# A two-layer hybrid decoder on one core: two of the four weight sums of a Strassen block by accumulating DMAs, ten such blocks, reordered projections, 512-column first up blocks

## The chip, the cores and the metric

One Trainium2 chip, of which the kernel uses one core. The metric is the device time of one execution in microseconds. The kernel before was timed in three runs: 949.24 us median, 949.19 to 950.22.

## The reference

Two decoder layers on a sequence of 256 tokens (T) with 1024 features (D), all in float32. Each layer ends with the MLP that most of the change touches:

```python
for l in range(DEPTH):                                 # DEPTH = 2
    u = rms_norm(h, norm_mix_pre[l])
    proj = u @ w_in[l]                                 # 1024 x 7680: q, k, v, xr, yr, pp, gates
    q, k, v, xr, yr, pp, gt = jnp.split(proj, SPLITS, axis=-1)
    ...                                                # attention, RG-LRU on xr and yr, pooling of pp, gates
    mix = merged @ w_out[l]
    h = h + rms_norm(mix, norm_mix_post[l])
    m = rms_norm(h, norm_mlp_pre[l])
    y = jnp.square(jax.nn.relu(m @ w_mlp_up[l])) @ w_mlp_down[l]     # 1024 -> 4096 -> 1024
    h = h + rms_norm(y, norm_mlp_post[l])
```

## The kernel before, in words

**Split products.** Every float32 product runs on TensorE as three products in a faster format (fp32r): high by high, high by low, low by high. `split` (L88 to L95) makes the two parts of a tile: ScalarE copies it rounded (L90, the high part), VectorE subtracts that from the source (L91, the low part). So each weight passes DMA, ScalarE and VectorE before TensorE reads it.

**Weights.** All large weights are laid out by the host as units of 128 x 1024 floats (512 KB) in the order of use, `wts`. `load_to` (L136) issues their loads on the SP queue (L140) into a ring of NRAW = 7 raw tiles; `split_to` splits them into rings of 8 high and 8 low tiles. The instructions are recorded in program order, with a few jobs put off by `later` and `tick` and some given a high priority; the tile scheduler then orders each engine's queue. An engine runs its queue in order.

**The projections.** pp, yr and xr take four units of work each per layer. `w_unit2` (L285 to L304) does one: two PSUM banks, each with eight matmuls of 512 columns (high weights against both parts of u, L299 and L302) and eight of 256 columns (low weights, L300). The 512 columns are two pieces of 256 in the tile `u2`.

**The MLP's up projection** is cut into 16 blocks of 256 hidden features. `up_first` (L733) does the first two with tokens as rows: per half of the tokens and per block `by_pass` (L330 to L339) runs 24 matmuls of 256 columns (L337), and the result is transposed into `zs`. Between its matmuls `mlp_in(1)` puts the transposes (L222) that bring the second half of the tokens into the feature layout. The other 14 blocks go through `up` (L764): `w_unit`, 48 matmuls of 256 columns (L98 to L100), relu and square.

**The MLP's down projection** has a block of 256 hidden features (two units of weights) for each up block. The first `nstr` = NBLK - PLAIN = 8 blocks use Strassen's form (Winograd's variant) for a 2 x 2 by 2 x 2 split: seven products of half size instead of eight. Seven PSUM banks collect the seven products over all blocks. For each block VectorE makes four sums of hidden pieces (`hidden_forms`, L777 to L780) and four sums of weight pieces (`weight_sums`): L794 adds the left half of the second unit to both halves of the first (1024 wide), L798 and L799 go on from there (512 wide each). Then `weight_forms` splits the four sums (`sh`, `sl`), and `down` runs 21 matmuls of 512 columns. UPS says how many up units stand ahead of each block's products: (2, 2, 2, 1, 2, 1, 2, 1). The other 8 blocks are plain: 24 matmuls of 512 columns each (`plain`); the last three of them (LAST) run together at the end. The weight sums lie in a tile of the `acts` pool under the tag "lo", which has two buffers.

Of the kernel before, what the change touches and what calls it, by code (L numbers as in the profile page):

```python
# [9 lines left out]
F32 = mybir.dt.float32  # L10
# [3 lines left out]
ALU = mybir.AluOpType  # L14
PSUM = bass.MemoryType.PSUM

L = 2
D = 1024
T = 256
P = 128  # L20
# [16 lines left out]
PLAIN = 8  # L37
LAST = 3

UPS = (2, 2, 2, 1, 2, 1, 2, 1)  # L40
NBLK = 16
# [17 lines left out]
def trunk(ctx, tc, x, wts, rgw, par, gpost, eye, ctab, out):  # L59
# [72 lines left out]

    per_layer = NHU // L
    fine = {i + l * per_layer for l in range(L) for i in [*range(FINE[0]), *range(per_layer - 64, per_layer - 64 + FINE[1])]}

    def load_to(n):  # L136
        while st["load"] < min(n, NHU):
            i = st["load"]
            r = raws.tile([P, HU_COLS], F32, tag="raw", name=f"raw{i}")
            nc.sync.dma_start(r[:], wts[i])  # L140
            raw_t[i] = r
            st["load"] += 1
# [144 lines left out]
    def w_unit2(hus, x2):  # L287


        banks = []  # L290
        for n in range(2):
            ps = bank([P, 2, T])
            for i, (wh, wl) in enumerate(hus):
                a = wh.rearrange("p (k n) -> p k n", k=4)
                b = wl.rearrange("p (k n) -> p k n", k=4)
                for k in range(4):
                    c = 4 * i + k
                    if c < 7:
                        PE.matmul(ps[:], a[:, k, n * P:(n + 1) * P], x2[:, :, c, :], start=c == 0, stop=False)  # L299
                    PE.matmul(ps[:, 0, :], b[:, k, n * P:(n + 1) * P], x2[:, 0, c, :], start=False, stop=False)  # L300
                    if c == 7:
                        PE.matmul(ps[:], a[:, k, n * P:(n + 1) * P], x2[:, :, c, :], start=False, stop=True)  # L302
            banks.append(ps)
        return banks  # L304
# [63 lines left out]
    for l in range(L):  # L368
# [361 lines left out]
        nstr = NBLK - PLAIN  # L730
        prods = {}
        zs, forms, wforms = {}, {}, {}

        def up_first():

            hus = take(4)
            toks = []
            for j in range(2):
                zs[j] = ttile([P, 2, T], nm="z")

            def hidden_T(tt):
                p2 = bank([P, 4, P])
                for j in range(4):
                    PE.transpose(p2[:, j, :], toks[tt][:, j * P:(j + 1) * P], ident)
                for j in range(2):
                    A.activation(zs[j][:, :, tt * P:(tt + 1) * P], p2[:, 2 * j:2 * j + 2, :], AF.Copy)

            for tt in range(2):
                ps = bank([P, 512])
                for u in range(2):  # L750
                    w = [[t_.rearrange("p (k n) -> p k n", k=4)[:, k, :] for hu in hus[2 * u:2 * u + 2]
                          for k in range(4) for t_ in hu[i:i + 1]] for i in range(2)]
                    by_pass(ps[:, u * 256:(u + 1) * 256], uh, ul, w[0], w[1], tt,
                            mid=(lambda: mlp_in(1)) if tt == 0 and u == 1 else None)
                z = ttile([P, 512], nm="zt")
                A.activation(z[:], ps[:], AF.Relu)
                V.tensor_tensor(out=z[:], in0=z[:], in1=z[:], op=ALU.mult)
                toks.append(z)
            later(1, lambda: hidden_T(0))
            later(1, lambda: hidden_T(1))  # L760
# [25 lines left out]

        def weight_sums(j):

            load_to(st["split"] + 2)
            r0, r1 = raw_t.pop(st["split"]), raw_t.pop(st["split"] + 1)  # L790
            st["split"] += 2
            st["use"] += 2
            t8 = acts.tile([P, 4, 512], F32, tag="lo", name="wsum")
            V.tensor_tensor(out=t8[:, 0:2, :], in0=r0.rearrange("p (b n) -> p b n", b=2),  # L794
                            in1=r1[:, 0:512].unsqueeze(1).to_broadcast([P, 2, 512]), op=ALU.add)
            w1 = (his.tile([P, HU_COLS], F32R, tag="wh", name="dh"), los.tile([P, HU_COLS], F32R, tag="wl", name="dl"))
            w4 = (ttile([P, 512], F32R, nm="bh"), ttile([P, 512], F32R, nm="bl"))
            V.tensor_tensor(out=t8[:, 2, :], in0=t8[:, 0, :], in1=r0[:, 512:1024], op=ALU.add)  # L798
            V.tensor_tensor(out=t8[:, 3, :], in0=t8[:, 2, :], in1=r1[:, 512:1024], op=ALU.add)  # L799
            split(w1[0][:], w1[1][:], r0[:])  # L800
            split(w4[0][:], w4[1][:], r1[:, 512:1024])
            wforms[j] = [w1, w4, t8]
            load_to(st["split"] + NRAW - 2)

        def weight_forms(j):
            t8 = wforms[j].pop()
            for i in range(2):
                w = (his.tile([P, HU_COLS], F32R, tag="wh", name="sh"), los.tile([P, HU_COLS], F32R, tag="wl", name="sl"))
                split(w[0][:], w[1][:], t8[:, 2 * i:2 * i + 2, :].rearrange("p b n -> p (b n)"))
                wforms[j].append(w)  # L810
# [12 lines left out]

        up_first()
        split_to(st["use"] + 2)
# [6 lines left out]
        for j in range(nstr):  # L832
            for i in range(UPS[j]):
# [110 lines left out]
def _layout(i):  # L944
    qc = np.concatenate([np.arange(hd * 64, hd * 64 + 64) for hd in _HEADS])
    units, rg, par, gp = [], [], [], []
    for l in range(L):
# [21 lines left out]
        units += [up[0], up[1], up[2], pairs[0], up[3]]  # L969
# [43 lines left out]
```

## Time and profile before

| | |
|---|---|
| median of three runs | 949.24 us |
| the profiled execution's own time | 949.69 us |
| its span | 947.9 us |
| TensorE (PE) busy | 936.9 us, 99% of the span |
| VectorE (DVE) busy | 751.6 us, 79% |
| ScalarE (ACT) busy | 624.9 us, 66% |
| GpSimd (POOL) busy | 2.0 us |
| weight loads on the SP queue | 316 of 512 KB, 4.4 us from issue to landing |

The profiled execution's time is 1.8 us more than its span, which begins with the first and ends with the last recorded work. A row of the profile names line, engine, operation and the tiles written and read. The durations of TensorE's rows overlap, since matmuls are pipelined: what one costs in a run is the distance between two starts.

### The profile page before, as it was taken

What the parts mean: (1) busy time and instruction counts of PE and PEld (TensorE: products, weight loads), DVE (VectorE), ACT (ScalarE), POOL (GpSimd) and SP (SyncE); (2) the same over time, 40 slices, a digit from 0 to 9 for tenths busy, and PEclk for the clock granted to TensorE, in tenths of its full rate; (3) what the DMA queues carried; (4) which work ended last, traced back from release to release, by engine and by line L of the source; (5) the groups of instructions that cost most, each with busy time, mean ns of one, the idle gap of its engine ahead of it and who ended that gap; (6) DMA issues with size and microseconds to landing.
All of it is one profiled execution on the core that took longest, in us unless ns stands there. A gap on an engine that the chain in (4) does not pass through costs nothing.

```text
span 947.9 us, 14352 instructions
## 1 busy us (share of the span) xinstructions
PE 936.9 (99%) x5284; PEld 805.1 (85%) x5284; DVE 751.6 (79%) x1321; ACT 624.9 (66%) x1079; POOL 2.0 (0%) x20
## 2 busy tenths in 40 slices
PE   8999999999999999999999999999999999999997
PEld 5888977888888999998878888888888899999985
DVE  6878886879868988886596788786897599889753
ACT  8655765679737777675375666656995478676731
POOL 0000000000000000000000000000000000000000
PEclk9999999999999999999999999999999999999998
DMA  8764454543754655566457545545438265656621
GB/s 321 275 213 160 134 182 163 194 159 125 268 176 154 215 178 189 200 201 221 134 182 259 165 144 181 184 140 192 155 125 287 100 221 184 230 171 200 214 72 44
DMA packets 48742, 173.24 MB, mean 183 GB/s; under 512 B 5408, under 2 KB 5792, under 8 KB 48672
## 3 DMA queue, kind: packets, MB, share of 16 engines
q1 hardware_dynamic: 48384, 172.16, 54.4%
q8 instruction: 41, 0.67, 0.3%
q14 instruction: 29, 0.24, 0.1%
q10 hardware_dynamic: 288, 0.17, 0.1%
HBM read 171.26 MB, written 1.05 MB: 182 GB/s over the span
## 4 chain that ended last, share of the span: by engine, by line
PE 98%; ACT 1%; DMA 1%; DVE 0%; issue 0%; SPq 0%; DVEq 0%
PE ps L98 17%; PE ps L100 17%; PE ps L99 17%; PE ps L337 9%; PE ps L299 8%; PE pr L98 6%; PE pr L99 6%; PE pr L100 6%; PE ps L300 5%; PE ps L425 1%; PE ps L473 1%; PE ps L302 1%; PE ps L462 1%; PE ps L222 1%; DMA raw<-wts 1%; PE ps L405 0%
## 5 line engine op out<-in xcount | busy, mean ns | idle before, releaser
L91 DVE TENSOR_TENSOR wl<-raw,wh 128x1024 fp32r<-128x1024 f32 (+1 forms) x312 | 344.8, 1124 | 78.1 <-ACT wh L90 69.7
L90 ACT ACTIVATE wh<-raw 128x1024 fp32r<-128x1024 f32 (+1 forms) x312 | 296.3, 987 | 145.6 <-PE ps L100 47.3
L98 PE MATMUL ps<-m,wh 128*128 128x256 f32 x448 | 126.8, 283 | 0.0
L100 PE MATMUL ps<-m,wl 128*128 128x256 f32 x448 | 126.8, 283 | 0.0
L99 PE MATMUL ps<-m,wh 128*128 128x256 f32 x448 | 126.7, 283 | 0.0
L299 PE MATMUL ps<-u,wh 128*128 128x512 f32 x336 | 121.1, 399 | 0.0
L300 PE MATMUL ps<-u,wl 128*128 128x256 f32 x384 | 99.9, 281 | 0.0
L98 PEld LDWEIGHTS ps<-m,wh 128*128 128x128 f32 x448 | 85.9, 192 | 1.0
L99 PEld LDWEIGHTS ps<-m,wh 128*128 128x128 f32 x448 | 85.9, 192 | 0.9
L100 PEld LDWEIGHTS ps<-m,wl 128*128 128x128 f32 x448 | 85.9, 192 | 0.0
L98 PE MATMUL ps<-wh,u 128*128 128x512 f32 x200 | 78.5, 393 | 0.5 <-ACT u L228 0.5
L100 PE MATMUL ps<-wh,u 128*128 128x512 f32 x200 | 78.0, 390 | 0.4 <-DVE u L230 0.4
L99 PE MATMUL ps<-wl,u 128*128 128x512 f32 x200 | 78.0, 390 | 0.0
L300 PEld LDWEIGHTS ps<-u,wl 128*128 128x128 f32 x384 | 72.5, 189 | 3.8
L299 PEld LDWEIGHTS ps<-u,wh 128*128 128x128 f32 x336 | 63.2, 188 | 14.2 <-issue 0.7
L98 PE MATMUL pr<-wh,hid 128*128 128x512 f32 x128 | 49.9, 390 | 0.0
L100 PE MATMUL pr<-wh,hid 128*128 128x512 f32 x128 | 49.8, 389 | 0.0
L99 PE MATMUL pr<-wl,hid 128*128 128x512 f32 x128 | 49.8, 389 | 0.0
L90 ACT ACTIVATE sh<-wsum 128x1024 fp32r<-128x1024 f32 x32 | 33.8, 1057 | 23.6 <-PE ps L99 20.5
L91 DVE TENSOR_TENSOR sl<-wsum,sh 128x1024 fp32r<-128x1024 f32 x32 | 38.9, 1222 | 11.7 <-ACT sh L90 11.3
L98 PEld LDWEIGHTS ps<-wh,u 128*128 128x128 f32 x200 | 37.5, 188 | 8.9 <-ACT u L228 0.7
L100 PEld LDWEIGHTS ps<-wh,u 128*128 128x128 f32 x200 | 37.5, 188 | 8.7 <-DVE u L230 0.9
(233 smaller groups left out, 1929.1 us busy)
## 6 DMA issues: line engine op xcount, KB each, us to landing
raw<-wts SPq DMA_DIRECT2D x316, 512.0 KB, 4.4
gB<-gpost SPq DMA_DIRECT2D x4, 512.0 KB, 5.5
rg<-rgw SPq DMA_DIRECT2D x8, 256.0 KB, 4.4
out<-h SPq DMA_DIRECT2D x4, 256.0 KB, 2.0
h<-x SPq DMA_DIRECT2D x2, 256.0 KB, 3.4
h<-x SPq DMA_DIRECT2D x1, 512.0 KB, 6.9
cst<-ctab SPq DMA_DIRECT2D x1, 168.0 KB, 7.0
prm<-par ACTq DMA_DIRECT2D x1, 104.0 KB, 3.8
```

The lines of the kernel that those rows point to most:

```text
L90: A.activation(hi, src, AF.Copy)
L91: V.tensor_tensor(out=lo, in0=src, in1=hi.bitcast(F32), op=ALU.subtract)
L98: PE.matmul(o, lh, rh, start=start, stop=False, **kw)
L99: PE.matmul(o, lh, rl, start=False, stop=False, **kw)
L100: PE.matmul(o, ll, rh, start=False, stop=stop, **kw)
L222: PE.transpose(banks[c // 4][:, c % 4, :], src[c // 4][:, (c % 4) * P:(c % 4 + 1) * P], ident)
L299: PE.matmul(ps[:], a[:, k, n * P:(n + 1) * P], x2[:, :, c, :], start=c == 0, stop=False)
L300: PE.matmul(ps[:, 0, :], b[:, k, n * P:(n + 1) * P], x2[:, 0, c, :], start=False, stop=False)
L302: PE.matmul(ps[:], a[:, k, n * P:(n + 1) * P], x2[:, :, c, :], start=False, stop=True)
L337: PE.matmul(o, xx[:, c, tsl], ww[c], start=(n == 0 and c == 0), stop=(n == 2 and c == 7))
L425: PE.matmul(sc[hd // hp][:, hd % hp, :], qT[a, j // 2][rows, j % 2, blk * P:(blk + 1) * P], kTs[0][rows, a, 0:w], start=True, stop=True)
L462: PE.transpose(ps[:, g, :], g8["p"](4 * b + g)[:, kt * P:(kt + 1) * P], ident)
```

## The change

- **Ten Strassen blocks** in a layer instead of eight (PLAIN 8 to 6); UPS becomes (2, 1, 1, 2, 1, 1, 2, 1, 1, 1), and the layout of the weights follows.
- **`dma_sums`**: for two blocks at a time, GpSimd's DMA queue loads the first unit of each into a tile `dsum` (L794) and then adds the left half of the second unit to both of its halves by a DMA with an add (L796). This takes the place of the 1024-wide add on VectorE. The tile is under the tag "lo", two buffers. It is called before and after `up_first` and at the start of every odd block for the pair three blocks on.
- The second unit's raw load brings its right half alone (256 KB); the two 512-wide sums (now L811, L812) go into a tile from the raw ring.
- **`w_unit2`** runs the eight matmuls of 512 columns of a bank first and the eight of 256 columns behind them.
- **`up_first`** runs one `by_pass` of 512 columns for each half of the tokens, with weights laid out for that; `mlp_in(1)` stays at the second matmul of the last pass of the first half.

```diff
@@ -34,10 +34,10 @@
-PLAIN = 8
+PLAIN = 6
 LAST = 3
 
-UPS = (2, 2, 2, 1, 2, 1, 2, 1)
+UPS = (2, 1, 1, 2, 1, 1, 2, 1, 1, 1)
@@ -130,6 +130,11 @@
+    nstr = NBLK - PLAIN
+    pair_at = [[(l + 1) * (NHU // L) - 64 + 6 + 2 * j + 2 * (sum(UPS[:j - 1]) + 1 if j else 0) for j in range(nstr)]
+               for l in range(L)]
+    half = {i + 1 for at in pair_at for i in at}
+
@@ -137,7 +142,10 @@
         while st["load"] < min(n, NHU):
             i = st["load"]
             r = raws.tile([P, HU_COLS], F32, tag="raw", name=f"raw{i}")
-            nc.sync.dma_start(r[:], wts[i])
+            if i in half:
+                nc.sync.dma_start(r[:, 512:1024], wts[i][:, 512:1024])
+            else:
+                nc.sync.dma_start(r[:], wts[i])
             raw_t[i] = r
             st["load"] += 1
 
@@ -290,16 +298,12 @@
         banks = []
         for n in range(2):
             ps = bank([P, 2, T])
-            for i, (wh, wl) in enumerate(hus):
-                a = wh.rearrange("p (k n) -> p k n", k=4)
-                b = wl.rearrange("p (k n) -> p k n", k=4)
-                for k in range(4):
-                    c = 4 * i + k
-                    if c < 7:
-                        PE.matmul(ps[:], a[:, k, n * P:(n + 1) * P], x2[:, :, c, :], start=c == 0, stop=False)
-                    PE.matmul(ps[:, 0, :], b[:, k, n * P:(n + 1) * P], x2[:, 0, c, :], start=False, stop=False)
-                    if c == 7:
-                        PE.matmul(ps[:], a[:, k, n * P:(n + 1) * P], x2[:, :, c, :], start=False, stop=True)
+            ws = [[hu[i].rearrange("p (k n) -> p k n", k=4)[:, k, n * P:(n + 1) * P] for hu in hus for k in range(4)]
+                  for i in range(2)]
+            for c in range(8):
+                PE.matmul(ps[:], ws[0][c], x2[:, :, c, :], start=c == 0, stop=False)
+            for c in range(8):
+                PE.matmul(ps[:, 0, :], ws[1][c], x2[:, 0, c, :], start=False, stop=c == 7)
             banks.append(ps)
         return banks
 
@@ -727,13 +731,14 @@
 
-        nstr = NBLK - PLAIN
-        prods = {}
+        prods, t8s = {}, {}
         zs, forms, wforms = {}, {}, {}
 
         def up_first():
 
             hus = take(4)
+            w = [[t_.rearrange("p (k n) -> p k n", k=2)[:, k, :] for hu in hus for k in range(2) for t_ in hu[i:i + 1]]
+                 for i in range(2)]
             toks = []
             for j in range(2):
                 zs[j] = ttile([P, 2, T], nm="z")
@@ -747,11 +752,7 @@
 
             for tt in range(2):
                 ps = bank([P, 512])
-                for u in range(2):
-                    w = [[t_.rearrange("p (k n) -> p k n", k=4)[:, k, :] for hu in hus[2 * u:2 * u + 2]
-                          for k in range(4) for t_ in hu[i:i + 1]] for i in range(2)]
-                    by_pass(ps[:, u * 256:(u + 1) * 256], uh, ul, w[0], w[1], tt,
-                            mid=(lambda: mlp_in(1)) if tt == 0 and u == 1 else None)
+                by_pass(ps[:], uh, ul, w[0], w[1], tt, mid=(lambda: mlp_in(1)) if tt == 0 else None)
                 z = ttile([P, 512], nm="zt")
                 A.activation(z[:], ps[:], AF.Relu)
                 V.tensor_tensor(out=z[:], in0=z[:], in1=z[:], op=ALU.mult)
@@ -784,29 +785,40 @@
             split(f[:, 0, 3:7, :], f[:, 1, 3:7, :], sm[:])
             forms[j] = f
 
+        def dma_sums(j0):
+
+
+            t = acts.tile([P, 2, 2, 512], F32, tag="lo", name="dsum")
+            js = range(j0, min(j0 + 2, nstr))
+            for j in js:
+                nc.gpsimd.dma_start(t[:, j - j0], wts[pair_at[l][j]].rearrange("p (b n) -> p b n", b=2))
+            for j in js:
+                nc.gpsimd.dma_start(t[:, j - j0], wts[pair_at[l][j] + 1][:, 0:512].unsqueeze(1).to_broadcast([P, 2, 512]),
+                                    accum_op=ALU.add)
+                t8s[j] = t[:, j - j0]
+
         def weight_sums(j):
 
             load_to(st["split"] + 2)
+            assert st["split"] == pair_at[l][j]
             r0, r1 = raw_t.pop(st["split"]), raw_t.pop(st["split"] + 1)
             st["split"] += 2
             st["use"] += 2
-            t8 = acts.tile([P, 4, 512], F32, tag="lo", name="wsum")
-            V.tensor_tensor(out=t8[:, 0:2, :], in0=r0.rearrange("p (b n) -> p b n", b=2),
-                            in1=r1[:, 0:512].unsqueeze(1).to_broadcast([P, 2, 512]), op=ALU.add)
+            t12 = t8s.pop(j)
+            t34 = raws.tile([P, 2, 512], F32, tag="raw", name="t34")
             w1 = (his.tile([P, HU_COLS], F32R, tag="wh", name="dh"), los.tile([P, HU_COLS], F32R, tag="wl", name="dl"))
             w4 = (ttile([P, 512], F32R, nm="bh"), ttile([P, 512], F32R, nm="bl"))
-            V.tensor_tensor(out=t8[:, 2, :], in0=t8[:, 0, :], in1=r0[:, 512:1024], op=ALU.add)
-            V.tensor_tensor(out=t8[:, 3, :], in0=t8[:, 2, :], in1=r1[:, 512:1024], op=ALU.add)
+            V.tensor_tensor(out=t34[:, 0, :], in0=t12[:, 0, :], in1=r0[:, 512:1024], op=ALU.add)
+            V.tensor_tensor(out=t34[:, 1, :], in0=t34[:, 0, :], in1=r1[:, 512:1024], op=ALU.add)
...
-            wforms[j] = [w1, w4, t8]
+            wforms[j] = [w1, w4, (t12, t34)]
             load_to(st["split"] + NRAW - 2)
 
         def weight_forms(j):
-            t8 = wforms[j].pop()
-            for i in range(2):
+            for t in wforms[j].pop():
                 w = (his.tile([P, HU_COLS], F32R, tag="wh", name="sh"), los.tile([P, HU_COLS], F32R, tag="wl", name="sl"))
-                split(w[0][:], w[1][:], t8[:, 2 * i:2 * i + 2, :].rearrange("p b n -> p (b n)"))
+                split(w[0][:], w[1][:], t.rearrange("p b n -> p (b n)"))
                 wforms[j].append(w)
 
         def down(j, part):
@@ -821,7 +833,9 @@
                 first, last = j == 0, j == nstr - 1 and p in (1, 5, 6, 7)
                 mm3(prods[p][:], f[:, 0, blk, :], f[:, 1, blk, :], w[0][:, cs], w[1][:, cs], first, last)
 
+        dma_sums(0)
         up_first()
+        dma_sums(2)
         split_to(st["use"] + 2)
         up(2)
         weight_sums(0)
@@ -830,6 +844,8 @@
         hidden_forms(0)
         nup = 3
         for j in range(nstr):
+            if j % 2 and j + 3 < nstr:
+                dma_sums(j + 3)
             for i in range(UPS[j]):
                 up(nup)
                 nup += 1
@@ -966,7 +982,7 @@
         dn = i["w_mlp_down"][l].reshape(NBLK, 2, P, D)
         nstr = NBLK - PLAIN
         pairs = [np.stack([np.concatenate([d[c][:, 512:], d[1 - c][:, :512]], 1) for c in range(2)]) for d in dn]
-        units += [up[0], up[1], up[2], pairs[0], up[3]]
+        units += [_s_units(i["w_mlp_up"][l][:, 0:512])[0], up[2], pairs[0], up[3]]
         nup = 3
         for j in range(nstr):
             for n in range(UPS[j]):
```

On VectorE, one Strassen block with one up unit, before (from the 1024-wide sum of block 4 of layer 0) and after (from the first 512-wide sum of block 3); `wl`, `dl`, `bl` and `sl` are low parts of weights, `sm` and `xf` the hidden sums and their parts, `t_` the tile of the two sums:

```order
L794 TENSOR_TENSOR wsum<-raw_3794,raw_3814 128x1024
L798 TENSOR_TENSOR wsum<-wsum,raw_3794 128x512
L91 TENSOR_TENSOR wl_3885<-raw_3709,wh_3884 128x1024
L799 TENSOR_TENSOR wsum<-wsum,raw_3814 128x512
L91 TENSOR_TENSOR wl_3889<-raw_3711,wh_3888 128x1024
L91 TENSOR_TENSOR bl<-raw_3631,bh 128x512
L777 TENSOR_TENSOR sm<-z 128x128
L778 TENSOR_TENSOR sm<-z 128x128
L779 TENSOR_TENSOR sm<-sm,z 128x128
L91 TENSOR_TENSOR sl<-wsum,sh 128x1024
L780 TENSOR_TENSOR sm<-z,sm 128x128
L91 TENSOR_TENSOR xf<-sm,xf 128x512
```

```order
L811 TENSOR_TENSOR t_3682<-dsum,raw_3473 128x512
L781 TENSOR_TENSOR sm<-z,sm 128x128
L812 TENSOR_TENSOR t_3682<-t_3682,raw_3475 128x512
L91 TENSOR_TENSOR dl<-raw_3473,dh 128x1024
L91 TENSOR_TENSOR xf<-sm,xf 128x512
L91 TENSOR_TENSOR xf<-z,xf 128x384
L91 TENSOR_TENSOR wl_3706<-raw_3575,wh_3705 128x1024
L91 TENSOR_TENSOR wl_3710<-raw_3595,wh_3709 128x1024
L91 TENSOR_TENSOR sl<-dsum,sh 128x1024
L91 TENSOR_TENSOR sl<-t_3682,sh 128x1024
L91 TENSOR_TENSOR bl<-raw_3475,bh 128x512
L778 TENSOR_TENSOR sm<-z 128x128
```

The 1024-wide sum from two raw tiles is gone, and the first sum now reads `dsum` and one raw tile.

On GpSimd, after, from the last memset of the mixer of layer 0 to the first one of layer 1:

```order
L625 MEMSET xr 128x2x3 x4
L794 DMA dsum<-wts 128x1024 x2
L796 DMA dsum<-wts 128x2x512 x2
L794 DMA dsum<-wts 128x1024 x2
L796 DMA dsum<-wts 128x2x512 x2
L794 DMA dsum<-wts 128x1024 x2
L796 DMA dsum<-wts 128x2x512 x2
L794 DMA dsum<-wts 128x1024 x2
L796 DMA dsum<-wts 128x2x512 x2
L794 DMA dsum<-wts 128x1024 x2
L796 DMA dsum<-wts 128x2x512 x2
L526 MEMSET xp 128x2x16 x4
```

Before, nothing stood between the memsets; now five groups of two loads and two adding DMAs do, each add behind the load of its own half of the tile.

On TensorE in `up_first` of layer 0, around the transposes of the second half of the tokens, before (line 222) and after (line 230):

```order
L337 MATMUL ps<-wh_3067,m 128x256 x4
L337 MATMUL ps<-wh_3061,m 128x256 x4
L337 MATMUL ps<-wh_3067,m 128x256 x4
L222 MATMUL ps<-idt,h 128x128 x4
L337 MATMUL ps<-wl_3062,m 128x256
L222 MATMUL ps<-idt,h 128x128 x4
L337 MATMUL ps<-wl_3062,m 128x256 x3
L337 MATMUL ps<-wl_3068,m 128x256 x4
L337 MATMUL ps<-wh_3043,m 128x256 x4
```

```order
L341 MATMUL ps<-wh_3072,m 128x512 x2
L341 MATMUL ps<-wl_3044,m 128x512 x2
L341 MATMUL ps<-wl_3050,m 128x512 x2
L341 MATMUL ps<-wl_3067,m 128x512
L230 MATMUL ps<-idt,h 128x128 x4
L341 MATMUL ps<-wl_3067,m 128x512
L230 MATMUL ps<-idt,h 128x128 x4
L341 MATMUL ps<-wl_3073,m 128x512 x2
L341 MATMUL ps<-wh_3043,m 128x512 x2
L341 MATMUL ps<-wh_3049,m 128x512 x2
```

The transposes stood behind 40 matmuls of 256 columns and now stand behind 21 of 512; behind the second group stood seven matmuls of 256 before the first that reads their result (`wh_3043` again), and now two of 512.

## Rows read from the trace of the kernel before

**Rows 1.** The page: busy time, share of the span and instructions of each engine; then the DMA's busy share in tenths in 40 equal slices; then the chain that ended last, by engine.

```profile
PE 936.9 (99%) x5284; PEld 805.1 (85%) x5284; DVE 751.6 (79%) x1321; ACT 624.9 (66%) x1079; POOL 2.0 (0%) x20
...
DMA  8764454543754655566457545545438265656621
...
PE 98%; ACT 1%; DMA 1%; DVE 0%; issue 0%; SPq 0%; DVEq 0%
```

**Rows 2.** TensorE's waits over the whole span: the waiting instruction's tile and line, what it waited for, then us in total, times, the longest in us.

```profile
PE ps L222 <- DVE un L349: 2.0, 2, 1.2
PE ps L126 <- DVE warm L123: 1.2, 1, 1.2
PE ps L98 <- ACT u L228: 0.5, 1, 0.5
PE ps L100 <- DVE u L230: 0.4, 1, 0.4
```

**Rows 3.** TensorE's timeline in the MLP of the first layer: start in us, duration in us, instruction and count. The first matmuls of an up unit, of its Strassen block, of the next up unit, of the last Strassen block, of the first plain block and of the second.

```profile
...
394.15 0.28 PE L98 MATMUL ps<-m,wh 128*128 128x256 f32 x1
...
399.91 0.40 PE L98 MATMUL pr<-dh,xf 128*128 128x512 f32 x1
...
404.73 0.28 PE L98 MATMUL ps<-m,wh 128*128 128x256 f32 x1
...
426.81 0.40 PE L98 MATMUL pr<-dh,xf 128*128 128x512 f32 x1
...
431.63 0.39 PE L98 MATMUL pr<-wh,hid 128*128 128x512 f32 x1
...
437.07 0.39 PE L98 MATMUL pr<-wh,hid 128*128 128x512 f32 x1
...
```

**Rows 4.** Busy time of the engines in three stretches: the start of the program, one up unit with its Strassen block, and 15 us of the Strassen stage. Columns: the stretch, its length, busy us and instructions of each engine, granted clock, DMA share, GB/s.

```profile
0.00:40.00 40.00, 35.87 (x158) 26.59 (x159) 32.25 (x94) 29.43 (x60) 0.45 (x6) 1.00 0.89 318
394.15:404.73 10.58, 10.58 (x70) 9.70 (x69) 10.16 (x15) 8.19 (x13) 0.00 (x0) 1.00 0.51 163
405.00:420.00 15.00, 15.00 (x113) 14.34 (x112) 11.44 (x16) 9.60 (x13) 0.00 (x0) 1.00 0.68 231
```

**Rows 5.** TensorE's timeline in the first up blocks of layer 0 (columns as above), up to the transposes that follow them; last, ScalarE's row of the copies into m that lies in it (in brackets the idle time before and what ended it).

```profile
298.95 2.08 PE L337 MATMUL ps<-wh,m 128*128 128x256 f32 x16
300.86 1.12 PE L337 MATMUL ps<-wl,m 128*128 128x256 f32 x8
301.82 2.08 PE L337 MATMUL ps<-wh,m 128*128 128x256 f32 x16
303.74 0.60 PE L222 MATMUL ps<-idt,h 128*128 128x128 f32 x4
304.09 0.36 PE L337 MATMUL ps<-wl,m 128*128 128x256 f32 x1
304.30 0.60 PE L222 MATMUL ps<-idt,h 128*128 128x128 f32 x4
304.65 1.07 PE L337 MATMUL ps<-wl,m 128*128 128x256 f32 x7
305.56 1.43 PE L337 MATMUL ps<-wh,m 128*128 128x256 f32 x8
306.83 0.28 PE L98 MATMUL ps<-m,wh 128*128 128x256 f32 x1
...
317.38 0.27 PE L744 MATMUL ps<-idt,zt 128*128 128x128 f32 x1
...
304.37 2.18 ACT L228 ACTIVATE m<-ps,prm 128x128 fp32r<-128x128 f32 x8 [2.52 <-PE ps L222]
```

**Rows 6.** TensorE's timeline in a projection unit: the end of one bank, the next bank from 93.33, and the start of the one after it.

```profile
93.09 0.40 PE L302 MATMUL ps<-u,wh 128*128 128x512 f32 x1
93.33 0.40 PE L299 MATMUL ps<-u,wh 128*128 128x512 f32 x1
93.56 0.28 PE L300 MATMUL ps<-u,wl 128*128 128x256 f32 x1
93.68 0.39 PE L299 MATMUL ps<-u,wh 128*128 128x512 f32 x1
...
95.91 0.40 PE L302 MATMUL ps<-u,wh 128*128 128x512 f32 x1
96.15 0.40 PE L299 MATMUL ps<-u,wh 128*128 128x512 f32 x1
```

**Rows 7.** VectorE's timeline at three places (columns as above, in brackets the idle time before and what ended it): the first sum of the first Strassen block, a 1024-wide sum followed by two splits, and a sum that waited.

```profile
...
304.02 1.22 DVE L794 TENSOR_TENSOR wsum<-raw,raw 128x1024 f32<-128x1024 f32 x1
...
339.57 1.22 DVE L794 TENSOR_TENSOR wsum<-raw,raw 128x1024 f32<-128x1024 f32 x1
340.71 2.35 DVE L91 TENSOR_TENSOR wl<-raw,wh 128x1024 fp32r<-128x1024 f32 x2
...
382.60 1.23 DVE L794 TENSOR_TENSOR wsum<-raw,raw 128x1024 f32<-128x1024 f32 x1 [1.16 <-DMA raw<-wts]
...
```

**Rows 8.** The raw weight tiles from 330 to 435 us: their DMA issues on SP, and the time from issue to landing.

```profile
L140 SPq DMA_DIRECT2D raw<-wts x39: 327/328/328, 335.2 to 433.4; - x39
...
DMA to landing us min/median/max: 3.3/4.4/7.0
```

**Rows 9.** TensorE's reads of the last tenant that a buffer of the dsum tile's tag has before the MLP: count, duration in ns (min/median/max), first and last start in us.

```profile
L100 PE MATMUL ps<-wh,rnl x32: 389/389/397, 252.9 to 274.9; 128*128 128x512 f32 x32
```

## The prediction

> **What bounds the kernel now.** I read the page's busy shares and its chain first [rows 1]. TensorE is busy 936.9 of 947.9 us and the chain that ended last is PE for 98%; the reader is to see that no other engine or transfer holds more than 1% of it. Second, TensorE's waits [rows 2]: four groups, 4.1 us in all, so there is next to no idle time to win, and a saving has to be matmul time. Third, because matmul rows overlap (a row of 512 columns lasts 0.39 us), I priced matmuls by start-to-start times in the timeline. In a plain block 24 matmuls of 512 columns start from 431.63 to 437.07 us, 0.227 us each; an up unit is 48 of 256 columns from 394.15 to 399.91, 0.120 us each [rows 3]. Fourth, what follows TensorE closely: VectorE in the Strassen stage is busy 10.16 of the 10.58 us of an up unit with one block [rows 4], so it is near its own bound there. Last, the DMA: 0.51 and 0.68 of its time in that stage, 0.89 in the first 40 us.
>
> The profiled execution took 949.69 us, 0.45 above the median of 949.24. The sum is made against it and then moved by those 0.45. About 0.2% (1.9 us) either way is what a measurement of this kernel can tell from no change.
>
> **Four blocks more in Strassen's form.** A Strassen block runs 21 matmuls of 512 columns (399.91 to 404.73 and 426.81 to 431.63, 4.82 us each), a plain one 24 in 5.44 us [rows 3]: 0.62 us less. Two blocks per layer, two layers: 4 x 0.62 = 2.5 us, all on TensorE's path. Bounds: 2.7 (12 matmuls at 0.227) if nothing is lost at the changeovers, and 0 or less only through the rivals below.
>
> **The first up blocks in 512 columns.** Per layer 96 matmuls of 256 columns become 48 of 512. At [rows 3] prices that is 96 x 0.120 = 11.5 against 48 x 0.227 = 10.9 us, 0.64 saved. Beyond that, this stretch holds small stalls. From 298.95 to 317.38 us TensorE ran 96 + 48 matmuls of 256 columns (17.3 us) and 8 transposes (about 0.7, from 303.74 to 304.09 for four): 18.0 of 18.43 us, so 0.45 is lost, most of it where 8 matmuls from 305.56 to 306.83 take 1.27 us instead of 0.96 [rows 5]. They wait piece by piece for the second half of m, which ScalarE copies from the transposes. After the change the transposes come after 21 matmuls of 512 columns, 4.76 us into the stretch, as now (4.79), so h comes no later for them; and a consumer that needs a new piece every 0.227 us instead of 0.120 is slower than ScalarE's 2.18/8 = 0.27 only slightly. I take 0.3 of the 0.45 as won: 0.95 per layer, 1.9 us together. Bounds 1.3 (only the columns) and 2.2. First the rows, then a rule that speaks against this: the rows give 0.120 and 0.227 us, so two halves cost 0.013 more than one whole. The Trainium skill ("TensorE: Matmul & The Clock Gate", section "Back-to-back issue gap") states a gap of N/2.4 + 2.5 ns, by which halving costs only those 2.5 ns; the term would shrink by about 1 us. The trace disagrees with it at both sizes, so I give it no chance of its own; its time, 945.3, lies inside the range.
>
> **The projections in two runs.** In 48 banks (12 units, 2 banks, 2 layers) eight matmuls of 512 and eight of 256 columns, now alternating, come as eight and eight. A bank takes 2.82 us now (93.33 to 96.15) [rows 6]. If each keeps its price in a run, 8 x 0.227 + 8 x 0.120 = 2.77. But where two of 512 columns with this two-piece operand follow each other, the start-to-start time is 0.24 (93.09 to 93.33, and the pair at 95.91), which gives 2.88. So a gain of 2.4 or a loss of 2.9 over 48 banks. The pair 0.23 + 0.12 inside a bank lies between; I take 0.01 per bank, 0.5 us gained.
>
> **What I cost at nothing.** VectorE loses the 1024-wide add of each block, 1.14 us start to start (339.57 to 340.71) of about 10.5 [rows 7], so an up unit with one block needs about 9.4 of TensorE's 10.58 us. The new order has up to three such units in a row, and this margin covers them; without it (the add staying) TensorE would be level with VectorE. ScalarE has 8.19 of 10.58 us [rows 4]. The old add also needed both raw tiles at once: at 382.60 it waited 1.16 us for a DMA, which TensorE did not feel [rows 7]. That wait's place goes to the first 512-wide add, which needs the summed tile and one raw tile. GpSimd, which now issues the DMAs, has 2.0 us of work in the whole span [rows 1], and its next memset is wanted in the following layer. The SP queue issues no more than before and half as many bytes for 20 of the units.
>
> **The accumulating DMA** is not in the old trace. Its chain per pair of blocks: wait until the tile's old sums are split, plain load, accumulate, complete. From the order, the closest pair (sums for blocks 4 and 5, after those of 1) has two up units with their blocks between release and first use, 2 x 10.58 = 21.2 us. A plain load of 512 KB lands in 3.3 to 7.0 us, 4.4 in the middle [rows 8]. The accumulate costs at least such a load again; above, I know no end from the trace. With two plain loads (say 7) and two accumulates at twice a load each in parallel (9) the chain is 16 us and hidden. For the first pair the tile is free when its former tenant was last read, near 274.9 us, and the old first sum started at 304.02: 29 us [rows 7, 9].
>
> The traffic: in two such units 21.2 us, 2.1 MB for the up units, 1.57 for the pairs, 1.05 plain and 1.05 accumulated: 5.77 MB, 272 GB/s. At the 0.0029 share per GB/s of [rows 4] (0.68 for 231) that is 0.80, below the 0.89 that the start shows. The Trainium skill ("Collectives: The Full Stack", section "The bandwidth ceiling: the fold count and why AG ≠ RS ≠ AR") says that an add in a DMA reads two sources and so runs at half a copy's rate; by it the demand would be 6.82 MB and the share 0.94. No run so far shows which it is; at 0.94 the first rival below would set in, whose chance takes this in.
>
> **Sum.** 2.5 + 1.9 + 0.5 = 4.9 us: 949.69 - 4.9 = 944.8 in such an execution, 944.3 on the median. With the bounds of the small terms (1.3 to 2.2, a part of 2.4 to -2.9) this case reaches 942.5 to 946.0; all of the projections' loss would be 947.7.
>
> **Rivals.**
> *The projections lose, or raw loads come late.* Either 0.06 us per bank (2.9) or, with the share near 0.8, waits of about 0.25 us in each of the 14 up units that carry a one-unit block: 3.5 us given back. For it: the add that waited 1.16 us at a share of only 0.5 to 0.7. Against: TensorE felt none of it. 946 to 949, about 947.8. Chance 0.12.
> *Slower: the accumulates don't keep up.* One mechanism, at the dsum tile of blocks 4 to 9 in each layer: the first 512-wide add of a block waits for the accumulate, VectorE stands with the splits behind it, and TensorE with VectorE. It decides where chain time exceeds the 21.2 us between release and use. With load and issue at 7 to 9 us that is an accumulate of 12 to 14 us, some three times a plain landing [rows 8]. At 16 us the closest pair loses 8 + 16 - 21.2, about 3; with 3 for each of the 6 refilled pairs (three per layer) that is 18, and 949.2 - 4.9 + 18 = 962. For it: 512-wide pieces instead of whole rows, sums made in place, and a DMA that has more to move than before. Against: two tiles, so a pair's sums are made while the other's are used. Chance 0.15.
> *More than expected.* The projections gain all 2.4 and the stalls go: 941.5 to 942.5. Chance 0.04.
> *The change does little.* If the new blocks' own start and end cost what they save (the plain blocks that are removed were also time in which VectorE caught up): 947.5 to 951. Chance 0.03.
> The forecast keeps 0.66.
>
> **How the numbers follow.** The forecast, the larger gain and the first rival together are 0.82, from 941.5 to 949.0: the range. Faster by over 0.2% (under 947.3): 0.66 + 0.04 + half of the first rival, 0.76. Within 0.2%: its other half and the last case, 0.09. Slower (over 951.1): 0.15.
>
> **What would show it.** In the profile after: the last Strassen block ends two blocks later and each replaced block takes 4.8 us; the 48 matmuls of the first up blocks start 0.227 us apart with at most 0.15 us lost; a projection bank takes 2.77 to 2.85 us; TensorE's waits stay near 4 us, and no wait of VectorE on the dsum tile's DMA passes to TensorE. The forecast is wrong if the waits show PE behind VectorE behind such a DMA, if landings of the accumulates are over 12 us, or if banks take over 2.87 us.

## The result and the profile after

The change takes 944.49 us in the median of six runs (943.82 to 944.80), the kernel before 949.59 beside it: a ratio of 0.9944, 95% interval 0.9933 to 0.9955, or 5.1 us less. The prediction was 944.3 with a range of 941.5 to 949.0. The span of the profiled execution fell from 947.9 to 942.8 us. One of the eleven runs of the projections alone, further down, took 1158.98 us at a granted clock of 0.753 where the ten others had 0.997 to 0.999, and it stays out of the ranges and ratios.

The page after: busy time of the engines, the DMA's share in tenths of 40 slices, the two large DMA queues (packets, MB, share of 16 engines' span), and the chain by engine.

```profile
PE 932.3 (99%) x5176; PEld 798.7 (85%) x5176; DVE 750.0 (80%) x1341; ACT 630.9 (67%) x1091; POOL 37.7 (4%) x60
...
DMA  8765445544776888858457544645438688987621
...
q1 hardware_dynamic: 48384, 166.92, 52.6%
q0 software_dynamic: 8320, 20.97, 9.9%
...
PE 98%; ACT 1%; DMA 1%; DVE 0%; issue 0%; SPq 0%; DVEq 0%
```

TensorE still holds 98% of the chain, as in [rows 1]. GpSimd went from 2.0 to 37.7 us and the DMA works more in the MLP stages, and neither appears in the chain. TensorE's waits after (waiting tile and line, what it waited for, us, times, longest):

```profile
PE ps L126 <- DVE warm L123: 1.2, 1, 1.2
PE ps L230 <- DVE un L353: 1.0, 2, 0.7
PE ps L98 <- ACT u L236: 0.8, 1, 0.8
PE ps L100 <- DVE u L238: 0.4, 1, 0.4
```

They are the four of [rows 2], 3.4 us against 4.1, and none names a sum. Where the time went can be read from the starts of matmuls. First the last Strassen block of layer 0, the first plain one and the second (start, duration):

```profile
435.19 0.40 PE L98 MATMUL pr<-dh,xf 128*128 128x512 f32 x1
...
439.99 0.39 PE L98 MATMUL pr<-wh,hid 128*128 128x512 f32 x1
...
445.43 0.39 PE L98 MATMUL pr<-wh,hid 128*128 128x512 f32 x1
```

4.80 us against 5.44, nearly as in [rows 3]. From the transposes behind the up blocks (L744 before, L749 after) to the last plain matmul of the layer the two traces differ by 1.36 us in layer 0 and 1.34 in layer 1, 2.7 together. Then the first up blocks of layer 0:

```profile
298.66 3.79 PE L341 MATMUL ps<-wh,m 128*128 128x512 f32 x16
...
305.00 3.81 PE L341 MATMUL ps<-wh,m 128*128 128x512 f32 x16
308.65 1.98 PE L341 MATMUL ps<-wl,m 128*128 128x512 f32 x8
310.46 0.28 PE L98 MATMUL ps<-m,wh 128*128 128x256 f32 x1
...
316.21 0.27 PE L749 MATMUL ps<-idt,zt 128*128 128x128 f32 x1
```

17.55 us where [rows 5] has 18.43: 0.88 less, in layer 1 as well. The 16 matmuls from 305.00 take 3.65 us, 0.228 each, so the slow 1.27 us of [rows 5] is gone. Last, a projection bank:

```profile
93.48 2.00 PE L304 MATMUL ps<-u,wh 128*128 128x512 f32 x8
95.32 1.12 PE L306 MATMUL ps<-u,wl 128*128 128x256 f32 x8
96.27 2.00 PE L304 MATMUL ps<-u,wh 128*128 128x512 f32 x8
```

2.79 us here against 2.82 in [rows 6]; in the mean of all 48 banks 2.815 against 2.839, 1.1 us in all. The three parts make 2.7 + 1.8 + 1.1 = 5.6 us; 0.3 went back before the first projection, which starts at 45.99 us after and 45.70 before (and anywhere from 45.2 to 46.4 in the kernels below), and 0.2 behind the last matmul, where 7.45 us follow instead of 7.24. Those 0.2 show in every kernel here that has the DMA sums and in none that has not.

### The profile page after: what moved, and what is told of

Same layout as the page of the kernel before. It is cut to its first block, busy times and chain, and to the rows that moved or that the text cites. A ratio compares the mean times of both kernels' runs of the same rounds, so it can differ in the third digit from the quotient of the medians.

```text
span 942.8 us, 14266 instructions
## 1 busy us (share of the span) xinstructions
PE 932.3 (99%) x5176; PEld 798.7 (85%) x5176; DVE 750.0 (80%) x1341; ACT 630.9 (67%) x1091; POOL 37.7 (4%) x60
## 3 DMA queue, kind: packets, MB, share of 16 engines
q1 hardware_dynamic: 48384, 166.92, 52.6%
## 4 chain that ended last, share of the span: by engine, by line
PE 98%; ACT 1%; DMA 1%; DVE 0%; issue 0%; SPq 0%; DVEq 0%
PE ps L98 18%; PE ps L99 17%; PE ps L100 17%; PE ps L304 9%; PE ps L341 9%; PE pr L98 6%; PE pr L99 6%; PE pr L100 6%; PE ps L306 5%; PE ps L429 1%; PE ps L477 1%; PE ps L466 1%; PE ps L230 1%; DMA raw<-wts 1%; PE ps L409 0%; PE ps L660 0%
## 5 line engine op out<-in xcount | busy, mean ns | idle before, releaser
L91 DVE TENSOR_TENSOR wl<-raw,wh 128x1024 fp32r<-128x1024 f32 (+1 forms) x304 | 333.5, 1123 | 67.0 <-ACT wh L90 57.7
L90 ACT ACTIVATE wh<-raw 128x1024 fp32r<-128x1024 f32 (+1 forms) x304 | 287.5, 987 | 127.1 <-PE ps L100 49.7
L100 PE MATMUL ps<-m,wl 128*128 128x256 f32 x448 | 126.9, 283 | 0.0
L304 PE MATMUL ps<-u,wh 128*128 128x512 f32 x384 | 96.9, 394 | 0.0
L100 PEld LDWEIGHTS ps<-m,wl 128*128 128x128 f32 x448 | 86.0, 192 | 0.0
L98 PE MATMUL ps<-wh,u 128*128 128x512 f32 x200 | 78.7, 393 | 0.8 <-ACT u L236 0.8
L100 PE MATMUL ps<-wh,u 128*128 128x512 f32 x200 | 78.0, 390 | 0.4 <-DVE u L238 0.4
L306 PEld LDWEIGHTS ps<-u,wl 128*128 128x128 f32 x384 | 52.4, 191 | 3.8
L306 PE MATMUL ps<-u,wl 128*128 128x256 f32 x384 | 53.5, 282 | 0.0
L98 PEld LDWEIGHTS ps<-wh,u 128*128 128x128 f32 x200 | 37.6, 188 | 9.3 <-ACT u L236 1.0
L100 PEld LDWEIGHTS ps<-wh,u 128*128 128x128 f32 x200 | 37.6, 188 | 8.6 <-DVE u L238 0.9
L99 PEld LDWEIGHTS ps<-wl,u 128*128 128x128 f32 x200 | 37.6, 188 | 7.7 <-DVE wl L91 0.4
L341 PE MATMUL ps<-wh,u 128*128 128x512 f32 x176 | 43.3, 394 | 0.0
L448 ACT ACTIVATE pr<-ps,s 128x128 f32<-128x128 f32 (+1 forms) x64 | 25.9, 430 | 25.8 <-DVE s L439 21.3
L341 PEld LDWEIGHTS ps<-wh,u 128*128 128x128 f32 x176 | 32.4, 188 | 7.9 <-ACT wh L90 0.9
L98 PE MATMUL pr<-wh,hid 128*128 128x512 f32 x96 | 37.5, 390 | 0.0
```

The costliest lines, as they stand in the source:

```text
L90: A.activation(hi, src, AF.Copy)
L91: V.tensor_tensor(out=lo, in0=src, in1=hi.bitcast(F32), op=ALU.subtract)
L98: PE.matmul(o, lh, rh, start=start, stop=False, **kw)
L99: PE.matmul(o, lh, rl, start=False, stop=False, **kw)
L100: PE.matmul(o, ll, rh, start=False, stop=stop, **kw)
L304: PE.matmul(ps[:], ws[0][c], x2[:, :, c, :], start=c == 0, stop=False)
```

## The experiments

Differences are to the kernel before as timed beside each: 949.36 us for the first four runs, 949.93 for the next four and 949.87 for the last four.

**Which part carries the gain.** Four kernels, each with one part alone or one part undone.

The sums on VectorE again, with the two 512-wide sums back in `wsum`, all else as in the change:

```diff
-            if i in half:
-                nc.sync.dma_start(r[:, 512:1024], wts[i][:, 512:1024])
-            else:
-                nc.sync.dma_start(r[:], wts[i])
+            nc.sync.dma_start(r[:], wts[i])
...
-            t12 = t8s.pop(j)
-            t34 = raws.tile([P, 2, 512], F32, tag="raw", name="t34")
+            t8 = acts.tile([P, 4, 512], F32, tag="lo", name="wsum")
+            t12, t34 = t8[:, 0:2, :], t8[:, 2:4, :]
+            V.tensor_tensor(out=t12, in0=r0.rearrange("p (b n) -> p b n", b=2),
+                            in1=r1[:, 0:512].unsqueeze(1).to_broadcast([P, 2, 512]), op=ALU.add)
...
-        dma_sums(0)
...
-        dma_sums(2)
...
-            if j % 2 and j + 3 < nstr:
-                dma_sums(j + 3)
```

> The change with its ten blocks, its projections and its first up blocks, but all four weight sums on VectorE again and the second unit loaded whole: no DMA on GpSimd's queue. Theory (the margin of VectorE is what the DMA sums buy): VectorE needs 10.5 us in an up unit with one block against TensorE's 10.58, so it falls behind where three such units follow each other; TensorE waits 0.2 to 0.5 us in some of the 14, 946 to 949 us. Rival 1 (the DMA sums buy nothing, the rings absorb it): 944.5 within 0.7. Rival 2 (the sums need both raw tiles at once and loads come late): waits of VectorE on raw tiles that pass to TensorE, above 950.

Measured: 944.57 us (944.26 to 944.93), ratio 0.995 (0.9937 to 0.9962). Rival 1: without the DMA sums the change is as fast as with them, within what these runs tell apart. My theory of a wait in several of the 14 units is wrong.

Eight blocks (`PLAIN = 8` and the old UPS), sums by DMA:

> The change with PLAIN and UPS as before: eight Strassen blocks, their sums by DMA. Theory (each block is 3 matmuls of 0.227 us fewer, nothing else): the change's 944.5 plus 4 x 0.675 = 2.7, so 947.2. Rival (the DMA sums themselves save or cost time on TensorE's path): off from 947.2 by more than 0.7.

Measured: 947.03 us (946.48 to 947.18), ratio 0.9974 (0.9963 to 0.9985), 2.3 less than before. The change saves 5.1, so the four blocks are worth 2.8 by the medians. The theory holds.

The kernel before with the change's `w_unit2` alone:

> The kernel before with the projections of the change alone. Theory (a bank is 0.024 us shorter, as the two traces show, 2.839 to 2.815 in the mean of 48): 949.5 - 1.15 = 948.4. Rival (the shorter bank belongs to something else, the projections change nothing): 949.5 within 0.3. My prediction's term was 0.5: 949.0.

Measured: 948.38 us (ten of eleven runs 947.92 to 949.01), ratio 0.9989 (0.998 to 0.9998). 1.0 us, as the traces said; my prediction's 0.5 was too small.

The kernel before with the change's `up_first` (and its weight layout) alone:

> The kernel before with the first up blocks of the change alone (48 matmuls of 512 columns in a layer). Theory: 0.88 us in each layer, 949.5 - 1.76 = 947.7. Rival (only the columns count, 0.64 in each layer, and the stall around the transposes stays): 948.2.

Measured: 948.23 us (948.02 to 948.66), ratio 0.9988 (0.9979 to 0.9997): 1.1 us, the rival's number but not its reason. The stretch itself is 0.84 and 0.82 us shorter than before; 0.28 is given back in the first Strassen block of each layer, and 0.84 + 0.82 - 2 x 0.28 is the 1.1 that was measured. TensorE's timeline in that block of layer 0, and after it VectorE's:

```profile
324.54 0.39 PE L99 MATMUL pr<-bl,xf 128*128 128x512 f32 x1
324.94 0.50 PE L100 MATMUL pr<-dh,xf 128*128 128x512 f32 x1
325.28 0.39 PE L100 MATMUL pr<-bh,xf 128*128 128x512 f32 x1
```

```profile
324.21 0.68 DVE L91 TENSOR_TENSOR xf<-sm,xf 128x512 fp32r<-128x512 f32 x1
```

Two starts that should be 0.227 apart are 0.40 and 0.34 apart; the first stands right behind the split that ends at 324.89. TensorE arrives at the block earlier than before (323.14 instead of 324.01 us), and VectorE does not (that split starts at 324.21, before at 324.19). The run with all sums on VectorE has the same two gaps, in both layers:

```profile
323.57 0.40 PE L99 MATMUL pr<-bl,xf 128*128 128x512 f32 x1
323.97 0.50 PE L100 MATMUL pr<-dh,xf 128*128 128x512 f32 x1
324.31 0.39 PE L100 MATMUL pr<-bh,xf 128*128 128x512 f32 x1
```

The change has none there: TensorE arrives at 322.83 and the split starts at 322.26. So the DMA sums do buy something in the trace, about 0.28 us in a layer, at its first Strassen block.

**The slower rival, with a larger dose.** Each adding DMA twice:

```diff
+                nc.gpsimd.dma_start(t[:, j - j0], wts[pair_at[l][j] + 1][:, 0:512].unsqueeze(1).to_broadcast([P, 2, 512]),
+                                    accum_op=ALU.add)
```

> The change with each adding DMA run twice in a row (the left half of the second unit is added twice, so two of the four sums have other values): the dose of the slower rival. Now a group of two loads and two adds takes 5 + 8 + 8 us, one add at a time, and the least slack before the first reader is 11.5 us. Theory (GpSimd's queue is in order, adds go one at a time): a group takes 5 + 4 x 8 = 37 us, while VectorE wants a group every 24 us, so from the third group on the reader waits; the five groups of a layer end 10 to 40 us late, 965 to 1020 us, and TensorE's waits grow by that. Rival (slack and two tiles absorb it): 944.5 to 946.

Measured: 994.87 us (991.3 to 997.24), ratio 1.047 (1.045 to 1.049). The largest waits of TensorE, and VectorE's on the DMA:

```profile
PE pr L98 <- ACT xf L90: 26.5, 4, 10.3
PE pr L100 <- DVE xf L91: 3.8, 6, 0.9
```

```profile
DVE t L813 <- DMA dsum<-wts: 75.0, 8, 14.5
```

VectorE's first sum of a block waits for the DMA eight times, 75 us, and TensorE stands behind the splits that follow. That is the rival's mechanism at its place; the change is below its threshold. A second cost shows from 350 to 430 us (busy us and instructions of PE, PEld, DVE, ACT and POOL; granted clock, DMA share, GB/s):

```profile
350.00:430.00 80.00, 65.31 (x398) 58.13 (x397) 48.43 (x70) 41.33 (x56) 13.15 (x13) 0.87 0.82 231
```

The granted clock is 0.87 in the mean, so for part of it TensorE ran at the lower of its two levels (1.2 of 2.4 GHz); it was busy 65.3 of those 80 us and stood still in between. Over the whole span it is busy 945.8 us instead of 932.3. In the kernels below that never pause, the same stretch shows 1.00.

**Why the adds go one at a time.** In the change the second add of a group is issued only when the first has landed. GpSimd's timeline for one group (start, duration, what it waited for):

```profile
377.89 1.13 POOL L794 DMA_DIRECT2D dsum<-wts  x2 [7.92 <-DVE sl L91]
382.76 1.24 POOL L796 DMA_DIRECT2D dsum<-wts  x1 [3.74 <-DMA dsum<-wts]
392.60 1.20 POOL L796 DMA_DIRECT2D dsum<-wts  x1 [8.61 <-issue]
```

"issue" means a wait that the profile does not name. The edit: `dynamic_dma_scratch_size` from 1024 to 6144.

> The change with six times the room for the descriptors that GpSimd writes for its DMAs (6144 instead of 1024). In the change the second add of a group is issued 0.3 us after the first has landed, some 8 us late. Theory (the room is full until then): both adds are issued within 1.5 us, and a group is done some 4 to 8 us earlier; the time stays at 944.5, since nobody waits for it. Rival (the adds go one at a time for another reason): the issues stay 8 us apart.

Measured: 945.08 us (943.72 to 945.55), ratio 0.9946 (0.9934 to 0.9959). The same group:

```profile
377.16 1.12 POOL L794 DMA_DIRECT2D dsum<-wts  x2 [17.60 <-DVE sl L91]
381.69 2.46 POOL L796 DMA_DIRECT2D dsum<-wts  x2 [3.41 <-DMA dsum<-wts]
```

Both adds leave within 2.5 us (over all groups their issues are 0.9 to 3.7 apart), the group is done at 394.7 instead of 401.6, and nobody waits for a sum: the medians, 0.6 apart, don't tell the two kernels apart. But two adds at a time can hold up other loads. In this profiled execution, at 945.55 us the slowest of the five, a raw tile issued at 772.30 us landed after 8.8 us, ScalarE waited 3.0 us for it, and TensorE lost 1.7 us in the first Strassen block of layer 1, which the change does not lose.

**More blocks.** If a block is worth 0.68 us and the sums are covered, more of them should pay. `PLAIN = 4`, `UPS = (2, 1, 1, 1, 1, 1, 1, 1, 1, 1, 1, 1)`, once in the change and once in the form with all sums on VectorE:

> The change with twelve Strassen blocks a layer (PLAIN 4, UPS 2 and then eleven times 1), sums by DMA. Theory (each block is worth 0.675 us as long as the adds keep up, and here they just do): 944.5 - 4 x 0.675 = 941.8. Rival (the group of 21 us meets a reader every 21.2 us, raw loads come late beside it, DMA share over 0.9): waits of VectorE for dsum or raw tiles that pass to TensorE, 943 to 955.

Measured: 941.42 us (941.01 to 941.84), ratio 0.9909 (0.9894 to 0.9924).

> Twelve Strassen blocks as in the run beside it, but all sums on VectorE as in the run with ten. Theory (VectorE's 10.5 us just fit in TensorE's 10.58, as with ten blocks): 944.5 - 2.7 = 941.9, within 0.7 of the other form. Rival (eleven units in a row leave no place to catch up): TensorE waits for VectorE's splits, 943 to 948, and here the DMA sums would pay.

Measured: 941.61 us (941.53 to 941.73), ratio 0.9913 (0.9899 to 0.9926). Both theories hold, although in the first form the adds now land only 6.0 us ahead of their closest reader, and in the second VectorE is busy 79.79 of 80 us.

`PLAIN = 3` and 13 ones in UPS, with `drain()` moved ahead of the joint plain blocks:

> Thirteen Strassen blocks a layer, one up unit ahead of each, sums by DMA; the three plain blocks left are the joint ones at the end, and the other four product banks are combined before them. Theory (a block is worth 0.675 us while VectorE and the adds keep up): 941.4 - 1.35 = 940.1. Rival (the streamed plain block was the time in which the last splits and the hidden parts were made): TensorE waits in front of the joint blocks, 1 us or more in each layer, 941.5 to 945.

Measured: 940.33 us (939.66 to 940.85), ratio 0.9901 (0.9887 to 0.9914), the fastest of all.

> Thirteen Strassen blocks as in the run beside it, all sums on VectorE. Theory (VectorE just fits beside TensorE in the blocks, and TensorE waits only if it is behind at their end): 940.3, within 0.7 of the DMA form. Rival (with twelve blocks VectorE was busy 79.8 of 80 us, it is behind at the end with nothing to catch up in): 942 to 946, and the DMA sums pay by 1.5 or more.

Measured: 941.11 us (940.53 to 941.73), ratio 0.9907 (0.9892 to 0.9922). 0.8 above the other form in the medians, with runs that overlap: just outside the theory's 0.7, and not the 1.5 or more of the rival.

**Where VectorE's bound is.** One 512-wide sum made twice in every block of the two kernels with twelve:

```diff
             V.tensor_tensor(out=t34[:, 1, :], in0=t34[:, 0, :], in1=r1[:, 512:1024], op=ALU.add)
+            V.tensor_tensor(out=t34[:, 1, :], in0=t34[:, 0, :], in1=r1[:, 512:1024], op=ALU.add)
```

> Twelve blocks, sums on VectorE, and one 512-wide add of each block made twice (same values), 0.60 us more VectorE work for each block. Theory (the margin of VectorE beside TensorE is 0.1 us, so this goes over it): 11.1 against 10.58 us in each of eleven units in a row, less a head start of 1 to 3 us in each layer: 941.6 + 2 x (2.5 to 5) = 946.5 to 951.5. Rival (VectorE's busy time has slack in it and is no bound): 941.6 to 942.5.

Measured: 942.18 us (942.03 to 943.32), ratio 0.9924 (0.9911 to 0.9936): 0.6 more than without it, where I expected 5 to 10. The rival's number came out.

> Twelve blocks, sums by DMA, with the same add made twice. Theory (the DMA sums buy VectorE 1.14 us a block, which is worth nothing until VectorE is over its bound, and then the whole excess): 10.0 against 10.58 us, so 941.4 to 942. Rival (what is short is something else, the order of VectorE's queue or the raw loads): as slow as the run beside it.

Measured: 941.83 us (941.39 to 942.09), ratio 0.9916 (0.9903 to 0.993), as the theory had it, with runs that overlap those of the other form. Busy time from 350 to 430 us (PE, PEld, DVE, ACT, POOL; clock, DMA share, GB/s) with twelve blocks: sums on VectorE, the same with the extra sum, and by DMA with the extra sum.

```profile
350.00:430.00 80.00, 80.00 (x520) 73.23 (x519) 79.79 (x116) 59.27 (x79) 0.00 (x0) 1.00 0.58 195
```

```profile
350.00:430.00 80.00, 80.00 (x519) 73.23 (x519) 80.00 (x119) 58.05 (x79) 0.00 (x0) 1.00 0.58 192
```

```profile
350.00:430.00 80.00, 80.00 (x520) 73.29 (x519) 76.91 (x117) 58.52 (x79) 10.65 (x12) 1.00 0.87 254
```

And in the second of these, VectorE from one block to the next:

```profile
388.65 1.22 DVE L91 TENSOR_TENSOR dl<-raw,dh 128x1024 fp32r<-128x1024 f32 x1
...
399.75 1.22 DVE L91 TENSOR_TENSOR dl<-raw,dh 128x1024 fp32r<-128x1024 f32 x1
```

The rate was priced right: a block takes VectorE 11.10 us against TensorE's 10.58, and VectorE never pauses, so the rival's reason (slack in its busy time) fails too. What I had wrong was the head start. Over the ten intervals between the eleven one-unit blocks VectorE loses 0.52 x 10, about 5 us, and TensorE is held up only at the end, by 0.25 us in layer 0 (438.68 us) and 0.33 in layer 1 (900.67). The head start is in weights that are split before they are read. First VectorE's split of an up unit's first low part at two places of layer 0, then TensorE's first reads of them (L100):

```profile
335.97 1.21 DVE L91 TENSOR_TENSOR wl<-raw,wh 128x1024 fp32r<-128x1024 f32 x1
...
437.67 1.22 DVE L91 TENSOR_TENSOR wl<-raw,wh 128x1024 fp32r<-128x1024 f32 x1
```

```profile
343.82 0.28 PE L100 MATMUL ps<-m,wl 128*128 128x256 f32 x1
...
438.68 0.28 PE L99 MATMUL ps<-m,wh 128*128 128x256 f32 x1
438.95 0.39 PE L100 MATMUL ps<-m,wl 128*128 128x256 f32 x1
```

The first split ends 6.6 us ahead of its reader, the last with it. Without the extra sum this lead stays at 6.7 to 7.8 us. So the 1.14 us a block that the DMA sums give VectorE buy nothing inside the blocks until the lead is used up; at 0.52 us a block over, eleven blocks just do that.

What the DMA sums are worth shows best from the first matmul of `up_first` in layer 0 to the end of the span, which leaves out the varying start of the program. With the sums on VectorE and by DMA this takes 644.65 and 644.16 us with ten blocks, 641.91 and 641.50 with twelve, 640.59 and 640.00 with thirteen, and 642.27 and 641.75 with twelve and the extra sum. That is one profiled execution each, but in all four pairs the DMA form is 0.4 to 0.6 us shorter: in the first three mostly the gaps at the first Strassen block of each layer, less the 0.2 behind the last matmul.

## Why the prediction was right, point by point

- **Four blocks more**: 2.5 predicted, 2.7 in the traces (the upper bound: 12 matmuls at 0.227), 2.8 by the medians with and without them. Right.
- **The first up blocks**: 1.9 predicted, 1.76 in the traces. The columns gave 0.64 a layer and the stall another 0.24 of its 0.45. The text compared the pace the wrong way round: a consumer every 0.227 us is faster than ScalarE's 0.27, not slower, but ScalarE starts 0.94 us ahead (304.06 against 305.00), and none of the 16 matmuls waits. The rule set against this term is one that the Trainium skill ("TensorE: Matmul & The Clock Gate", section "Back-to-back issue gap") gives for a single matmul by itself. The rows are of a stream with a weight load before each matmul, so they do not speak against it. Alone the term is 1.1, since VectorE then holds up the first Strassen block of each layer; inside the change it is whole because the DMA sums free VectorE there. My text priced the parts apart and did not see that one leans on the other.
- **The projections**: 0.5 predicted, 1.1 in the traces and 1.0 alone. The term was mis-sized: in a run of eight the two-piece matmul starts every 0.230 us (93.48 to 95.32), not the 0.24 that I had weighed in from the bank's end in [rows 6].
- **What was costed at nothing** cost nothing, but three reasons were wrong. "Without it TensorE would be level with VectorE" was right in rate and missed the head start: with all sums on VectorE ten blocks take 944.57 us. "Two accumulates in parallel" was wrong: they go one at a time, so a group takes 20 to 24 us (24 from 377.89 to 401.55), not 16. And the closest pair has 25.0 us between the release of its tile (328.23) and its first use (353.27), not 21.2. It stays hidden, because the first block of a pair needs only its own add, here landed at 341.78, and the second is read one block later. The smallest slack between an add's landing and its reader is 11.5 us.
- **The DMA**: landings of raw tiles from 330 to 435 us went from 4.4 to 5.2 us in the middle and from 7.0 to 7.6 at most. From 360 to 375 us its share was 0.89 at 242 GB/s, so bytes cost more than the 0.0029 of the prediction. Estimated from the queue lines above: q1 costs 52.6 / 166.92 = 0.315% of the span per MB; if q0's 10.5 MB of plain loads cost the same, its 10.5 MB of adds cost 0.63%, twice as much. The trace's packets show it directly: a plain packet of 4 KB took 195 ns on q0 and 194 on q1 in the mean, a plain one of 2 KB 91 (q1), an adding one of 2 KB 193 (q0). That agrees with the rule of the Trainium skill ("Collectives: The Full Stack", section "The bandwidth ceiling: the fold count and why AG ≠ RS ≠ AR"), given there for the adds of collectives, that an add reads two sources and so runs at half a copy's rate. It did not bring the first rival: TensorE's waits name no raw tile.
- **The slower rival**: the mechanism exists (75 us of waits with the adds doubled), its threshold lies above the change.

The sum came out at 4.9 against 5.1. Its terms measured 5.6 in the traces: two were too small (2.5 for 2.7, 0.5 for 1.1) and one a little too large (1.9 for 1.8). That the sum is closer than its terms is luck, since the 0.5 that went back at the start and the end of the program was in no term.

## What to carry to other kernels

When one engine is busy all the time, price a change by that engine's start-to-start times. Work taken from an engine behind it is worth only the waits that it ends (here 0.28 us at the first Strassen block of a layer), until that engine's lag uses up its head start (here 6.6 us), and a rate alone does not tell when. The test is to undo the offload and keep the rest: here the accumulating DMAs looked like the main idea, and about 0.5 us of the 5.1 is theirs. A part measured alone can be worth less than inside the whole (1.1 against 1.76), because the engine it arrives early at is late.

## What the runs showed of the hardware

The adding DMAs of the change (occurrences, ns on GpSimd for each issue as min/median/max, first and last start in us; then issue to landing):

```profile
L796 POOL DMA_DIRECT2D dsum<-wts x20: 1197/1210/1238, 280.9 to 855.1; - x20
...
DMA to landing us min/median/max: 6.5/7.7/10.1
```

- They move 512 KB each in 7.7 us in the middle, one at a time; the plain loads of the same size and queue, issued two at a time, took 4.0 to 8.9, 6.2 in the middle, and 0.57 us of GpSimd each. An adding packet of 2 KB took 193 ns in the mean, a plain one 91.
- With 1024 for the descriptors' room the adds of a group are issued 7 to 10 us apart, with 6144 0.9 to 3.7 us apart; two at a time the later one lands 8 to 13 us after its issue.
- Waits cost TensorE twice here: with the adds doubled it stood still for 14.7 of 80 us and was granted 0.87 in the mean (1.00 in the kernels without waits), and it was busy 13.5 us longer over the span.
